# A first stage in sixteen groups of one K tile, finer attention preparation and another load order in a one-core mixer block

## The chip, the cores and the metric

The kernel runs on one core of one Trainium2 chip. The metric is the device time of one execution in microseconds; the kernel before takes 1273.27 us (median of three runs, 1273.0 to 1273.49). All times and rows in this document come from such runs and from the profile of one execution.

## What is computed

One layer of a hybrid block over 512 latent tokens that also reads 256 context tokens, all in 32-bit floats, width 2048:

```python
mod = silu(c) @ w_ada + b_ada                        # shift, scale, gate: 3 x 2048
h  = rms_norm(x, norm_w) * (1 + scale) + shift      # 512 tokens
hc = rms_norm(ctx, norm_w) * (1 + scale_c) + shift_c # 256 tokens, modulated by c_ctx
p, pc = h @ w_in, hc @ w_in                        # 6688 columns
# group A: gated delta rule, 8 heads, forward and backward scans in chunks of 64, after a short conv
# group B: attention, 8 query heads on 2 key heads, RMS norm of q and k, 2-D rotary positions
y = concat(gdn * silu(z_g), attn * silu(z_a)) @ w_out
out = rms_norm(x + gate * y, final_norm_w)
```

The modulation needs `shift` and `scale` before anything can be projected, and each of the sixteen K tiles (128 of the 2048 features) of `h` needs only its own 128 columns of `shift` and `scale`, but those columns over all 2048 rows of `w_ada`.

## The kernel before

Large products are made in three passes of rounded parts (`hi*hi`, `hi*lo`, `lo*hi`), so each weight piece is split by ScalarE (`hi`) and by GpSimd or VectorE (`lo`), and `h` is held as `hh` (high) and `hl` (low), with features on the partitions.

**First stage** (lines 307 to 567). The six token blocks of `ctx` and `x` are loaded (1 MB each), squared on ScalarE, turned by TensorE (`turn`, L363) and copied to `xts`. `ada(g)` (L388) makes shift and scale for a pair of K tiles: four 1 MB tiles `wada`, each filled by two transfers of 512 KB whose rows are 1 KB (256 columns), sixteen products of 512 columns (L404) into four column groups of 32 of the array, a copy (`part`, L409), four transposes (L413) and small VectorE steps into `md`. `make_h(g)` (L437) makes `hf = x * scale * 1/rms` (L446, VectorE), `hh` (L448, ScalarE) and `hl` (L450, VectorE) for both K tiles. `project(k)` (L463) adds one K tile to five accumulators (k, q of heads 0 and 1, v of head 0) in fifteen 512-column and nine 256-column passes, and yields after each of its five outputs. `gate_sums` (L453) adds the gate columns. The loop at L543 goes over eight groups of two K tiles: while group g is projected, `ada(g + 1)` and `make_h(g + 1)` are put into chosen slots of the ten. TensorE runs in the order in which this is written (`manual_schedule`); the other engines are ordered by the framework, SyncE issues all transfers in one queue. Six tiles of 1 MB (`big`) hold first the token blocks and then the `wada` pieces.

**Middle.** From the end of the first stage on, `pull(n)` puts about n columns of later projections on TensorE, between the links of other chains (L1228 to L1262). Then eight scans run, each with 35 slots; `prep_at` says at which slot the preparation of the next head goes on by one part. In the last scan `attn_prep` (L1044) is run in this way, at the slots of `LATE_AT`: fifteen parts that load, turn, normalise and rotate the keys, the values and the first query head. One part of it normalises and rotates a whole block on VectorE, and two scale a whole rotary table.

**Attention and output.** Thirteen `M` tiles are loaded, eight of the scans' outputs and then five z projections. In seventeen turns `u` the attention runs beside the z projection's fillers (`fill`) and the gate rows. `merged(i)` splits `M[i]` for the output product; all sixteen calls stand in the first output block.

```python
steps = ((3, 5, 6), (2, 5, 6), (2, 4, 5), (3, 5))[min(g, 3)]
sums = 0 if g + 1 == NG else steps[-1] if g < 2 else steps[0]
LATE_AT = dict.fromkeys((*range(1, 28, 2), 33), 1.5)
```

Of the kernel before, what the change touches and what calls it, by code (L numbers as in the profile page):

```python
# [17 lines left out]
D = 2048  # L18
# [4 lines left out]
NZA = 5  # L23
# [46 lines left out]
def build(tc, a):  # L70
# [23 lines left out]
    xts, hls = {}, {}  # L94
# [5 lines left out]

    def hl(m, k):
        return hls[m, k // 2][:, k % 2]
# [285 lines left out]
    def ada(g, halves=False):  # L388

        n, k0, rows = 2, 2 * g, 4  # L390
        md = mds[g] = p0.tile([128, 2, 2, 2], F32, tag="md", bufs=4, name=f"md{g}")

        def vec(v):
            return v[:, k0:k0 + n].unsqueeze(2).to_broadcast([128, n, 2])

        ada_ps = gtile([128, 512], f"ada{g}")
        for j in range(KT // rows):
            wt = big([128, rows, 2, 256], f"wada{g}_{j}")
            for s in range(2):
                src = w_ada[j * rows * 128:(j + 1) * rows * 128, s * D + k0 * 128:s * D + k0 * 128 + 256]  # L400
                SY.dma_start(wt[:, :, s], src.rearrange("(k p) c -> p k c", p=128))
            for r in range(rows):
                kk = j * rows + r
                T.matmul(ada_ps[32 * r:32 * r + 32], lhsT=cs[:, kk], rhs=wt[:, r].rearrange("p s c -> p (s c)"),  # L404
                         start=kk < 4, stop=kk >= KT - 4, skip_group_check=True)
            if j == 1 and halves:
                yield
        part = p0.tile([128, 512], F32, tag="part", bufs=2, name=f"part{g}")
        V.tensor_copy(part, ada_ps)  # L409
        yield  # L410
        tp = gtile([128, 4, 128], f"adat{g}")
        for i in range(4):
            T.transpose(out=tp[:, i], in_=part[:, i * 128:(i + 1) * 128], identity=ident)  # L413
        V.tensor_reduce(out=md.rearrange("p s i m -> p (s i) m"),
                        in_=tp.rearrange("p a (g m) -> p a m g", g=4)[:, :, 0:2], axis=AX.X, op=ALU.add)
        V.tensor_tensor(out=md[:, 0], in0=md[:, 0], in1=vec(vT), op=ALU.add)
        V.tensor_tensor(out=md[:, 1], in0=md[:, 1], in1=vec(b1), op=ALU.add)
        mul(V, md[:, 1], md[:, 1], vec(vT[:, 48:64]))

    wg = p0.tile([128, KT, 32], F32, name="wg")  # L420
# [14 lines left out]
    hfs = {}  # L435

    def make_h(p_):  # L437

        md = mds[p_]
        for m_ in range(2):  # L440
            hls[m_, p_] = low_tile(m_, p_, F32R, "h")
        for i in range(2):
            k = 2 * p_ + i
            hf = hfs[k] = p0.tile([128, NTOK], F32, tag="hf", bufs=3, name=f"hf{k}")
            for m_, t0, t1 in ((0, 0, SEQ), (1, SEQ, NTOK)):
                V.scalar_tensor_tensor(out=hf[:, t0:t1], in0=xts[m_, p_][:, i], scalar=md[:, 1, i, m_:m_ + 1],  # L446
                                       in1=rb[:, t0:t1], op0=ALU.mult, op1=ALU.mult)
                S.activation(hh[m_][:, k], hf[:, t0:t1], AF.Identity, bias=md[:, 0, i, m_:m_ + 1])  # L448
            for m_, t0, t1 in ((0, 0, SEQ), (1, SEQ, NTOK)):
                V.scalar_tensor_tensor(out=hl(m_, k), in0=hfs[k][:, t0:t1], scalar=md[:, 0, i, m_:m_ + 1],  # L450
                                       in1=hh[m_][:, k], op0=ALU.add, op1=ALU.subtract)

    def gate_sums(p_):  # L453

        for i in range(2):
            k = 2 * p_ + i
            for j in range(3):
                T.matmul(gps[32 * j:32 * j + 32], lhsT=wg[:, k], rhs=hfs[k][:, 256 * j:256 * j + 256],
                         start=False, stop=k == KT - 1, skip_group_check=True)
            T.matmul(gps[96:128, 0:2], lhsT=wg[:, k], rhs=mds[p_][:, 0, i], start=False, stop=k == KT - 1,  # L460
                     skip_group_check=True)
# [57 lines left out]
    for t in range(6):  # L519
        rds.append(turn(t))  # L520
        if t == 1:
            vec_columns()
        if t:
            spread(t - 1, rds[t - 1])
        if t == 4:
            first = ada(0, True)
            next(first)
    spread(5, rds[5])
    next(first)
    next(first, None)  # L530
    for k in range(2):
        first_weights(k)
    SY.dma_start(wg, w_in[:, COL_G:COL_G + 32].rearrange("(k p) c -> p k c", p=128))
    make_h(0)
# [8 lines left out]
    for g in range(NG):  # L543
        slot = 0
        ahead = ada(g + 1, g < 3) if g + 1 < NG else gates_in()
        steps = ((3, 5, 6), (2, 5, 6), (2, 4, 5), (3, 5))[min(g, 3)]
        sums = 0 if g + 1 == NG else steps[-1] if g < 2 else steps[0]
        for k in (2 * g, 2 * g + 1):
            if k + 2 < KT:
                first_weights(k + 2)  # L550
# [4 lines left out]
            for _ in project(k):  # L555
                if g + 1 < NG:
                    if slot in steps:
                        next(ahead, None)
                        if slot == steps[-1]:
                            make_h(g + 1)  # L560
# [1162 lines left out]
```

## Time and profile before

| | us |
|---|---|
| median of three runs | 1273.27 |
| the profiled execution | 1274.02 |
| its span, first to last instruction | 1271.9 |
| TensorE busy | 1235.5 (97%) |
| VectorE busy | 853.9 |
| ScalarE busy | 570.1 |
| first stage, to its last projection pass | about 158 |

The profile names an instruction by its line, its engine and the tiles that it writes and reads. PE is TensorE's matmul, PEld its weight load, DVE is VectorE, ACT ScalarE, POOL GpSimd, SP SyncE. A timeline row is: start in us, duration in us, engine, line, operation, output and inputs, shapes, count, and in brackets the idle time before it and what ended it. A busy PE isn't PE at its peak, since matmuls overlap: the distance between the starts of two passes is what a pass costs.

### The profile page before, as it was taken

Reading aid. Unit: us, or ns where it says so; the run is one execution under the profiler, and the core shown is the slowest. Engines: PE = TensorE matmul, PEld = TensorE weight load, DVE = VectorE, ACT = ScalarE, POOL = GpSimd, SP = SyncE. Lnnn points to the kernel's source line nnn. Section 1 sums busy time; section 2 is a strip of 40 time slices with the busy share of each in tenths; the row PEclk is TensorE's granted clock in tenths of the full one; section 3 lists DMA queues with packets and bytes.
Section 4 is the critical chain, followed back from the end, with each engine's and each line's share of the span. In section 5 each row is a group of like instructions: output and inputs, shape, how many; then the busy total and the mean of one; then the engine's idle time right before and its main releaser. Section 6 shows DMA issues by size and latency. Waiting matters only on the chain.

```text
span 1271.9 us, 24265 instructions
## 1 busy us (share of the span) xinstructions
PE 1235.5 (97%) x9242; PEld 1016.2 (80%) x9242; DVE 853.9 (67%) x1905; ACT 570.1 (45%) x1452; POOL 156.8 (12%) x206
## 2 busy tenths in 40 slices
PE   6899999999999999999999999999999999999997
PEld 4566788888888888888888887877888888787886
DVE  5444597596876778677786655547998997555433
ACT  5222373445545454454545444545555443434211
POOL 1222100111111111121211112200000000000000
PEclk9899999999999999999999999999999999999999
DMA  9999524132332223322233444357454443565202
GB/s 354 318 332 346 155 75 109 48 72 61 76 72 78 60 64 67 78 65 64 68 64 78 101 112 146 101 161 240 137 153 125 136 130 100 183 225 193 96 33 99
DMA packets 227287, 164.52 MB, mean 129 GB/s; under 512 B 62243, under 2 KB 198524, under 8 KB 226148
## 3 DMA queue, kind: packets, MB, share of 16 engines
q1 hardware_dynamic: 226874, 162.87, 44.1%
q8 instruction: 73, 1.20, 0.4%
q14 instruction: 43, 0.34, 0.1%
q10 hardware_dynamic: 297, 0.11, 0.0%
HBM read 148.85 MB, written 14.08 MB: 128 GB/s over the span
## 4 chain that ended last, share of the span: by engine, by line
PE 79%; DVE 10%; DMA 4%; ACT 3%; issue 3%; SPq 0%; POOL 0%; ACTq 0%; POOLq 0%; DVEq 0%
PE zl L1462 9%; PE kl L185 5%; PE ql L185 4%; PE vl L185 4%; PE po L148 3%; PE po L147 3%; PE po L149 3%; PE kvl L185 3%; PE tsh L972 3%; PE kx L185 2%; PE ada L404 2%; PE vx L185 2%; PE tsh L956 2%; PE klat L471 2%; PE pt L1391 2%
## 5 line engine op out<-in xcount | busy, mean ns | idle before, releaser
L960 ACT ACTIVATE vsh<-tsh,cch 128x128 f32<-128x128 f32 x88 | 32.4, 368 | 226.7 <-PE tsh L956 226.7
L289 POOL TENSOR_TENSOR sdh<-sth,egl 128x256 f32<-128x256 f32 x80 | 70.7, 884 | 445.2 <-DVE sth L978 364.3
L951 DVE SCALAR_TENSOR_TENSOR rh<-ksh,negeg,vtokh 64x128 f32<-64x128 f32 x176 | 61.2, 347 | 24.1 <-PE ksh L939 18.0
L148 PE MATMUL po<-wlo_wo,mh 128*128 128x512 f32 x192 | 76.1, 396 | 0.2 <-DVE wlo_wo L131 0.2
L147 PE MATMUL po<-whi_wo,mh 128*128 128x512 f32 x192 | 76.1, 397 | 0.0
L149 PE MATMUL po<-whi_wo,ml 128*128 128x512 f32 x192 | 76.0, 396 | 0.0
L1462 PE MATMUL zl<-hhL,whi_z 128*128 128x512 f32 x176 | 71.4, 405 | 0.0
L1462 PE MATMUL zl<-hL,whi_z 128*128 128x512 f32 x176 | 69.7, 396 | 0.0
L1462 PE MATMUL zl<-hhL,wlo_z 128*128 128x512 f32 x176 | 69.4, 395 | 0.0
L131 DVE TENSOR_TENSOR wlo_wo<-wraw_wo,whi_wo 128x512 fp32r<-128x512 f32 x48 | 33.0, 689 | 51.2 <-ACT whi_wo L130 51.1
L978 DVE TENSOR_TENSOR sth<-sdh,tsh 128x256 f32<-128x256 f32 x80 | 33.7, 421 | 44.0 <-PE tsh L972 35.7
L130 ACT CAST whi_wo<-wraw_wo 128x512 fp32r<-128x512 f32 x48 | 29.7, 618 | 57.8 <-PE po L149 47.5
L972 PE MATMUL tsh<-vsh,ktok 128*128 128x128 f32 x352 | 54.3, 277 | 0.4 <-ACT vsh L960 0.4
L972 PEld LDWEIGHTS tsh<-vsh,ktok 128*128 128x128 f32 x352 | 48.0, 191 | 3.5 <-ACT vsh L960 0.6
L1036 ACT CAST pth<-pt 128x512 fp32r<-128x512 f32 x48 | 26.5, 586 | 44.3 <-PE pt L1391 44.3
L185 PE MATMUL vl<-hhL,whi_v 128*128 128x512 f32 x112 | 46.3, 413 | 0.0
L967 ACT ACTIVATE oqh<-ksh,egsw 64x128 f32<-64x128 f32 x128 | 45.9, 358 | 0.8
L185 PE MATMUL vl<-hhL,wlo_v 128*128 128x512 f32 x112 | 46.2, 413 | 0.0
L185 PE MATMUL vl<-hL,whi_v 128*128 128x512 f32 x112 | 45.6, 408 | 0.0
L1510 DVE SCALAR_TENSOR_TENSOR gacc<-graw,scol,gacc 128x512 f32<-128x512 f32 x60 | 44.9, 748 | 1.1
L147 PEld LDWEIGHTS po<-whi_wo,mh 128*128 128x128 f32 x192 | 36.1, 188 | 9.6 <-ACT ze L1416 0.8
L148 PEld LDWEIGHTS po<-wlo_wo,mh 128*128 128x128 f32 x192 | 36.1, 188 | 9.2 <-DVE wlo_wo L131 0.6
(545 smaller groups left out, 3901.0 us busy)
## 6 DMA issues: line engine op xcount, KB each, us to landing
wada<-in_w_ada SPq DMA_DIRECT2D x64, 512.0 KB, 8.6
graw<-in_w_ada SPq DMA_DIRECT2D x64, 256.0 KB, 3.0
wraw_wo<-in_w_out SPq DMA_DIRECT2D x48, 256.0 KB, 3.0
wraw_z<-in_w_in SPq DMA_DIRECT2D x44, 256.0 KB, 3.0
wraw_v<-in_w_in SPq DMA_DIRECT2D x28, 256.0 KB, 3.1
wraw_k<-in_w_in SPq DMA_DIRECT2D x24, 256.0 KB, 2.9
wraw_q<-in_w_in SPq DMA_DIRECT2D x24, 256.0 KB, 2.8
xs<-in_x SPq DMA_DIRECT2D x4, 1024.0 KB, 8.4
```

What stands on the lines that cost most here:

```text
L131: (lo_eng or G).tensor_tensor(out=lo, in0=raw, in1=hi, op=ALU.subtract)
L147: T.matmul(out, lhsT=lh, rhs=rh, start=start, stop=False, skip_group_check=True)
L148: T.matmul(out, lhsT=lh, rhs=rl, start=False, stop=False, skip_group_check=True)
L149: T.matmul(out, lhsT=ll, rhs=rh, start=False, stop=stop, skip_group_check=True)
L185: T.matmul(out, lhsT=lw, rhs=rt[m], start=k == 0 and n == 0, stop=k == KT - 1 and n == 2, skip_group_check=True)
L289: eng.tensor_tensor(out=out, in0=x, in1=y, op=ALU.mult)
L951: behind["DVE"] = V.scalar_tensor_tensor(out=r[rows], in0=ks[rows, d], scalar=gsc["negeg"][rows, gcol:gcol + 1], in1=vtok[rows, p], op0=AL ...
L967: S.activation(oq[rows, v, p - 2], ks[rows, d], AF.Copy, scale=gsc["egsw"][rows, gcol:gcol + 1])
L972: T.matmul(ts[:, d], lhsT=ktok[:, p, half], rhs=vs, start=True, stop=True, skip_group_check=True)
L978: behind["DVE"] = V.tensor_tensor(out=sn, in0=sd, in1=ts[:, 0:2], op=ALU.add)
L1462: T.matmul(pl, lhsT=lw, rhs=rt, start=k == 0 and m == 0, stop=k == KT - 1 and m == 2, skip_group_check=True)
L1510: V.scalar_tensor_tensor(out=acc, in0=raw, scalar=scol[:, k:k + 1], in1=acc, op0=ALU.mult, op1=ALU.add)
```

## The change

The first stage goes over sixteen groups of one K tile. For each, two transfers of 1 MB bring the 128 columns of scale and then the 128 columns of shift, in rows of 512 bytes. `ada(k)` makes the scale first, and `hf` with it, and then the shift, `hh` and `hl`: two times sixteen products of 128 columns, two copies, two single transposes. The steps are taken one per slot of `project`, and `gate_sums` is called for each K tile. `hl` of K tile 0 gets tiles of its own (`spare`), the others move up by one half tile, and the squares' unused output goes to a part of `hhL`. The attention's preparation is cut into more parts at other slots, the rotary tables are scaled in parts of their own, and the loads stand further ahead of their use. The z tiles of `M` are loaded alternately with the others, `merged(0)` is called in turn 12, and three fillers are put ahead of the last turn's third transposition. Two `pull` amounts change.

```diff
+    spare = [pool_.tile([128, n], F32R, name=f"h{s}spare") for pool_, n, s in lows]
     def hl(m, k):
-        return hls[m, k // 2][:, k % 2]
+        if k == 0:
+            return spare[m]
+        g = (k - 1) // 2
...
-        junk = p0.tile([128, D], mybir.dt.bfloat16, tag="junk", bufs=1, name=f"junk{t}")
+        junk = hhL[:, 12:16].rearrange("p k t -> p (k t)")
...
+    def load_ada(k, s):
+        wt = big([128, KT, 128], f"wada{k}_{s}")
+        c0 = s * D + k * 128
+        SY.dma_start(wt, w_ada[:, c0:c0 + 128].rearrange("(k p) c -> p k c", p=128))
+        pieces[k, s] = wt
+    def ada(k):
+        md = mds[k] = p0.tile([128, 2, 2], F32, tag="md", bufs=4, name=f"md{k}")
+        bank = gtile([128, 4, 128], f"ada{k}")
+        for s in (1, 0):
+            wt = pieces.pop((k, s))
+            for kk in range(KT):
+                r = kk % 4
+                T.matmul(bank[32 * r:32 * r + 32, s], lhsT=cs[:, kk], rhs=wt[:, kk], start=kk < 4, stop=kk >= KT - 4,
+                         skip_group_check=True)
+            part = p0.tile([128, 128], F32, tag="part", bufs=2, name=f"part{k}_{s}")
+            V.tensor_copy(part, bank[:, s])
+            yield
+            tp = bank[:, 2 + s]
+            T.transpose(out=tp, in_=part, identity=ident)
+            V.tensor_reduce(out=md[:, s], in_=tp.rearrange("p (g m) -> p m g", g=4)[:, 0:2], axis=AX.X, op=ALU.add)
+            if s:
+                V.tensor_scalar(out=md[:, 1], in0=md[:, 1], scalar1=b1[:, k:k + 1], scalar2=vT[:, 48 + k:49 + k],
+                                op0=ALU.add, op1=ALU.mult)
+                hf = hfs[k] = p0.tile([128, NTOK], F32, tag="hf", bufs=3, name=f"hf{k}")
+                for m_, t0, t1 in SPANS:
+                    V.scalar_tensor_tensor(out=hf[:, t0:t1], in0=xts[m_, k // 2][:, k % 2], scalar=md[:, 1, m_:m_ + 1],
+                                           in1=rb[:, t0:t1], op0=ALU.mult, op1=ALU.mult)
+            else:
+                V.tensor_scalar(out=md[:, 0], in0=md[:, 0], scalar1=vT[:, k:k + 1], scalar2=None, op0=ALU.add)
+                for m_, t0, t1 in SPANS:
+                    S.activation(hh[m_][:, k], hfs[k][:, t0:t1], AF.Identity, bias=md[:, 0, m_:m_ + 1])
+                for m_, t0, t1 in SPANS:
+                    V.scalar_tensor_tensor(out=hl(m_, k), in0=hfs[k][:, t0:t1], scalar=md[:, 0, m_:m_ + 1],
+                                           in1=hh[m_][:, k], op0=ALU.add, op1=ALU.subtract)
+            yield
...
+    load_ada(0, 1)
+    first_weights(0)
+    load_ada(0, 0)
+    first = ada(0)
+    next(first)
     spread(5, rds[5])
+    load_ada(1, 1)
+    load_ada(1, 0)
+    first_weights(1)
     SY.dma_start(wg, w_in[:, COL_G:COL_G + 32].rearrange("(k p) c -> p k c", p=128))
+    load_ada(2, 1)
+    load_ada(2, 0)
+    for _ in first:
+        pass
+    load_ada(3, 1)
+    load_ada(3, 0)
...
+    events = (e for k in range(1, KT) for e in ada(k))
+    for k in range(KT):
+        if k + 2 < KT:
+            first_weights(k + 2)
...
+        if k and k + 3 < KT:
+            load_ada(k + 3, 1)
+            load_ada(k + 3, 0)
+        for slot, _ in enumerate(project(k)):
+            if k == KT - 1:
+                if slot == 0:
+                    gate_sums(k)
+                if slot in (1, 4):
+                    with tc.high_priority(offset=2500):
+                        next(last, None)
+                continue
+            if slot or k == 0:
+                next(events, None)
+            if k == 0 and slot == 4:
+                next(events, None)
+            if slot == 0 and k:
+                gate_sums(k - 1)
+            if k == KT - 2 and slot == 3:
+                gate_sums(k)
...
-    LATE_AT = dict.fromkeys((*range(1, 28, 2), 33), 1.5)
+    LATE_AT = dict.fromkeys((0, *range(4, 15), *range(16, 30), 31), 1.5)
...
-    pull(22000)
+    pull(25500)
...
-    for n in (5000, 5500, 0, 0, 5500, 0, 4000, 0, 0, 14000, 0, 0, 0, 0, 0):
+    for n in (2500, 5500, 0, 0, 5500, 0, 4000, 0, 0, 14000, 0, 0, 0, 0, 0):
...
     for i in range(8):
+        if i < NZA:
+            SY.dma_start(M[8 + i], zad[i])
         SY.dma_start(M[i], o_d[i])
-    for i in range(NZA):
-        SY.dma_start(M[8 + i], zad[i])
...
+        if h >= NH:
+            fill(3)
         if before is not None:
             pts.append(attn_pt(before[0], before[1], before[2], 2))
...
+        if u == 2 * NH - 4:
+            merged(0)
...
-            if first:
+            if first and k:
                 merged(k)
```

In `attn_prep` the parts of one key block are now, in this order: turn and square two blocks; turn and square four blocks and load the values; scale the cosine table (first block only); scale the sine table (first block only); normalise the context keys; normalise the latent keys and make the swapped product; turn the context values; finish the rotation; turn the latent values and load the next block; turn back the keys in two parts. The first query head follows in five parts and a last one for its transposition.

More of the change, by code (lines that the diff above doesn't have):

```diff
@@ L386, in build @@
     mds = {}
[L388 to L418, printed above, removed]
@@ new lines, in build @@
+    pieces = {}
+    def load_ada(k, s):
[33 more added lines that the diff above has]
+            yield
@@ L433, in first_weights, with gate_sums @@
         w0[k] = (hi[:, 0], vhi, hi[:, 1]), (lo[:, 0], vlo, lo[:, 1])
[L435 to L461, printed above, removed]
+    def gate_sums(k):
+        for j in range(3):
+            T.matmul(gps[32 * j:32 * j + 32], lhsT=wg[:, k], rhs=hfs[k][:, 256 * j:256 * j + 256],
+                     start=False, stop=k == KT - 1, skip_group_check=True)
+        T.matmul(gps[96:128, 0:2], lhsT=wg[:, k], rhs=mds[k][:, 0], start=False, stop=k == KT - 1,
+                 skip_group_check=True)
     def project(k):
@@ L1080, in attn_prep, with scaled @@
-        parts = ((0, 2), (2, 4))
+            jk = NT[:, 0:2].rearrange("p a b -> p (a b)")
+            for t in range(n):
+                S.activation(jk, tp[:, t], AF.Square, accum_out=ss[:, t:t + 1])
+            V.tensor_scalar(out=ss[:, :n], in0=ss[:, :n], scalar1=1.0 / 128.0, scalar2=EPS, op0=ALU.mult, op1=ALU.add)
+            power(ss[:, :n], -0.5)
+            return ss[:, :n].unsqueeze(2).to_broadcast([128, n, 128])
+        def scaled(out, tp, r):
+            V.tensor_tensor(out=out, in0=tp, in1=r, op=ALU.mult)
@@ L1081, in attn_prep, with rope_one, rope_two @@
+        def rope_one(y, tb, nm):
+            t2 = gp.tile([128, 6, 128], F32, tag="vtok", bufs=2, name=f"rt2{nm}")[:, :4]
+            mul(V, t2.rearrange("p t (a s r) -> p (t a) s r", a=2, s=2), swapped(y),
+                tb[:, 1].rearrange("p t (a s r) -> p (t a) s r", a=2, s=2))
+            return t2
+        def rope_two(y, tb, t2):
+            mul(V, y, y, tb[:, 0])
+            V.tensor_tensor(out=y, in0=y, in1=t2, op=ALU.add)
         kn = ktoks[0].rearrange("p a s d -> p (a s) d")
+        rope_load(tabk)
@@ L1470, in fillers, with merged @@
         z_over(*over)
+    def merged(i):
+        if i >= 1:
+            mh.append(mp.tile([128, SEQ], F32R, name=f"mh{i}"))
+            ml.append(mp.tile([128, SEQ], F32R, name=f"ml{i}"))
+        S.copy(mh[i], M[i])
+        V.tensor_tensor(out=ml[i], in0=M[i], in1=mh[i], op=ALU.subtract)
     def gate_bias(acc, row):
```

140 lines of the change are left out of this document (62 added, 78 removed).

## The prediction

> **What bounds the kernel now.** I read the page first, then a table of stretches (columns: length, busy time of PE, PEld, DVE, ACT, POOL with counts, granted TensorE clock, share of the 16 DMA engines, GB/s), then timelines.
>
> ```profile
> PE 1235.5 (97%) x9242; PEld 1016.2 (80%) x9242; DVE 853.9 (67%) x1905; ACT 570.1 (45%) x1452; POOL 156.8 (12%) x206
> ```
> ```profile
> 18.00:28.00 10.00, 7.01 (x44) 3.41 (x42) 5.76 (x21) 4.46 (x8) 2.08 (x4) 0.88 1.08 350
> 38.00:92.00 54.00, 52.62 (x321) 33.87 (x321) 24.93 (x46) 14.14 (x30) 14.37 (x14) 0.94 1.10 347
> 97.00:137.00 40.00, 39.27 (x256) 27.33 (x258) 20.49 (x43) 11.12 (x24) 12.45 (x11) 1.00 1.09 348
> 140.00:158.00 18.00, 18.00 (x121) 14.07 (x114) 9.81 (x27) 4.89 (x9) 1.64 (x10) 1.00 0.18 45
> 171.00:172.00 1.00, 1.00 (x9) 0.91 (x9) 0.47 (x2) 0.41 (x3) 0.00 (x0) 1.00 1.13 337
> ```
>
> TensorE is the bound after the first stage, so a hole removed there is time gained, and a stage that ends later costs its delay in full. In the first stage two things run level: the transfers flow at 347 GB/s from 38 to 137 us, and TensorE is busy at the same time. When the transfers have ended, 18 us of projection still follow. The stage runs from the first to the last of these two passes, 38.61 to 158.04 us, 119.4 us:
>
> ```profile
> 38.61 0.50 PE L471 MATMUL klat<-hhL,whi_w 128*128 128x512 f32 x1 [3.51 <-ACT hhL L448]
> ...
> 158.04 0.40 PE L185 MATMUL kvl<-hhL,whi_kv 128*128 128x512 f32 x1
> ```
>
> What does TensorE need in it? The timeline gives the price of each part.
>
> ```profile
> 60.47 0.40 PE L471 MATMUL qlat<-hhL,wlo_w 128*128 128x512 f32 x1
> 60.80 1.92 PE L404 MATMUL ada<-wada,cs 128*32 128x512 f32 x16
> ...
> 62.99 0.28 PE L473 MATMUL cctx<-hhC,w0h 128*128 128x256 f32 x1
> ...
> 113.64 0.60 PE L413 MATMUL adat<-cmain,part 128*128 128x128 f32 x4
> 114.00 0.48 PE L471 MATMUL klat<-hhL,whi_w 128*128 128x512 f32 x1
> ...
> 148.20 0.42 PE L458 MATMUL cctx<-hf,wg 128*32 128x256 f32 x3
> ...
> 149.53 0.28 PE L473 MATMUL cctx<-hhC,whi_w 128*128 128x256 f32 x1
> ...
> 152.80 0.40 PE L471 MATMUL klat<-hhL,whi_w 128*128 128x512 f32 x1
> ...
> 156.54 0.28 PE L473 MATMUL cctx<-hhC,w0l 128*128 128x256 f32 x1
> ```
> ```profile
> 107.36 3.64 PE L404 MATMUL ada<-wada,cs 128*32 128x512 f32 x32
> ```
>
> A projection: four of its five outputs take 152.80 to 156.66, 3.86 us, the fifth 0.70 (three passes 0.235 apart), so 4.56 us per K tile. A run of ada passes: 32 in 3.64 us on four column groups is 0.43 us for each 512-column pass of a group, 0.21 for 256, 0.107 for 128 if it scales. From the end of the qlat pass (60.47 + 0.235) to the moment the next cctx pass could have followed at the usual distance (62.99 - 0.235) are 2.05 us, of which 4 x 0.43 stream: **0.34 us go on changing from whole-array passes to column groups and back, whatever the run's length.** The gate sums show the same: 1.2 us to 149.3, of which 0.85 stream. Four transposes cost 0.43 us, 0.107 each, with no such loss.
>
> Now: 16 x 4.56 = 73.0; seven pairs of ada streaming 3.41 = 23.9; ten runs' changes 3.4 (the first three pairs are in two runs); gate sums 8 x 0.85 + four changes = 8.2 (four others join an ada run); transposes 3.0; the gates' own transposes 0.57. Together 112.1 us. The clock takes 3.1 us more:
>
> ```profile
> 40.00:50.00 10.00, 10.00 (x43) 7.10 (x44) 2.39 (x3) 1.64 (x5) 2.81 (x4) 0.69 1.10 351
> ```
>
> (10 x 0.31). So 4.2 of the 119.4 us are waits, the level race with the transfers.
>
> **The start of the stage.** Scale and shift of one K tile need 2 MB instead of 4 MB, and the sixth token block's turn no longer stands behind a wait for them.
>
> ```profile
> 21.66 2.07 DVE L372 COPY xL<-xt 128x256 f32<-128x256 f32 x6
> ...
> 27.56 2.66 PE L363 MATMUL xt<-cmain,xs 128*128 128x128 f32 x16
> ...
> 28.72 2.42 DVE L372 COPY xL<-xt 128x256 f32<-128x256 f32 x7 [2.96 <-PE xt L363]
> ```
> ```profile
> L446 DVE SCALAR_TENSOR_TENSOR hf<-xL,md,rb 128x512 f32<-128x512 f32 x16 | 12.1, 754 | 0.4
> L448 ACT ACTIVATE hhL<-hf,md 128x512 fp32r<-128x512 f32 x16 | 11.6, 723 | 29.7 <-DVE hf L446 29.7
> ```
>
> The turn that now starts at 27.56 can start when VectorE's copies let it, about 22.5; VectorE, free at 23.7, needs 2.4 for its copies and is done at 26.2. At 350 GB/s from 18 us on, the scale piece is there at 21.0 and, behind the first weights (0.33 MB), the shift piece at 24.9, about a microsecond more to land: neither is late. Then: copy of the scale sums (a quarter of a copy that now takes 0.69, I take 0.25), transpose, reduction and factor to about 27.2; hf 0.75 and about 0.5 to 28.5; copy, transpose, reduction and addition of the shift 0.9; hh 0.72: **the first projection at about 30.3 instead of 38.61, 8.3 us earlier** (29 to 32).
>
> **What TensorE does after it.** Projections 73.0. Ada: 30 runs (15 K tiles, scale and shift) of 8 passes per column group, 0.853 + 0.34 = 1.19 each, 35.7. Single transposes 30 x 0.107 = 3.2. Gate sums sixteen times alone, 0.43 + 0.34 = 0.77 each, 12.3. Gates 0.57. Together 124.8, 12.7 more than now: the streaming is the same, but 46 changes of the array's form are paid where 14 were. The slow clock lies between 0 and 3.1 (TensorE idles less ahead of the start, but not none): I take 2. Waits: between 1 and 6, I take 3. Of them about 1.5 because the third K tile's weights now stand behind two pieces of 1 MB (K tiles 2 and 3) in SyncE's queue, and ScalarE's and GpSimd's split follows; 0.5 for the gates' transposes, whose VectorE copies now have three slots instead of six; the rest for the copies behind hl on VectorE, whose steps per K tile sum to under 4 of some 8 us. Each step has one output, 0.70 to 1.05 us, between a run and its transpose.
>
> **End of the stage: 30.3 + 124.8 + 2 + 3 = 160.1 instead of 158.0, 2.1 us later.** The transfers don't set this. The row at 171 us, two loads of the attention's weights with rows of 512 bytes like the new pieces, ran at 337 GB/s where 1 KB rows give 347, so the 33.6 MB cost 99.6 instead of 96.7 us, 2.9 more, and end near 141; behind the last piece stand one run, three outputs, two gate sums, a projection and the gates, some 10.5 us: 151.5. The other bound for them is the last rival. The 1 MB size by itself I cost at nothing: several transfers are under way at any time, which keeps 347 GB/s up already. The squares' output in hhL costs nothing: that part is first written by K tile 12.
>
> **The later parts.** These are TensorE's holes, by the timeline:
>
> ```profile
> 170.15 1.03 PE L596 MATMUL gcp<-gg__116,ctri 128*128 128x6 f32 x8 [1.06 <-DVE gg__116 L589]
> ...
> 769.11 0.46 PE L956 MATMUL tsh<-rh,UU 128*128 128x128 f32 x2 [1.02 <-DVE rh L951]
> 779.82 0.44 PE L1041 MATMUL vtp<-cmain,kvch 128*128 128x128 f32 x2 [0.62 <-DMA kvch<-kvd]
> ...
> 805.91 0.44 PE L1041 MATMUL vtp<-cmain,kvch 128*128 128x128 f32 x2 [0.48 <-DMA kvch<-kvd]
> 828.40 0.46 PE L956 MATMUL tsh<-rh,UU 128*128 128x128 f32 x2 [0.89 <-DVE rh L951]
> ...
> 870.59 0.66 PE L1391 MATMUL pt<-cmain,pr 128*128 128x128 f32 x4 [0.83 <-ACT qn L1334]
> 873.73 0.66 PE L1391 MATMUL pt<-cmain,pr 128*128 128x128 f32 x4 [0.38 <-DVE ptl L1037]
> 884.92 1.31 PE L1391 MATMUL pt<-cmain,pr 128*128 128x128 f32 x8 [0.94 <-DVE pr L1383]
> ...
> 1070.38 0.65 PE L1391 MATMUL pt<-cmain,pr 128*128 128x128 f32 x4 [1.02 <-DVE ptl L1037]
> ```
> ```profile
> 869.43 0.63 ACT L1567 ACTIVATE zae<-M 128x512 f32<-128x512 f32 x1 [2.88 <-DMA M<-zad]
> ...
> 882.91 0.61 ACT L1599 CAST mh<-M 128x512 fp32r<-128x512 f32 x1
> ```
>
> *The pulls.* 3500 more columns (about 1.6 us) stand before the gates' product; the gates' last copies begin about a slot later against the stage's end. Of 1.06 us I take 0.5 (0 to 1.06).
> *The last scan.* Four holes, 3.0 us. Two end with the scan's step rh, late behind a rotary table's scaling or a whole normalisation on VectorE; with one such product or pair per part, nothing over some 1.4 us stands before rh. Two end with the load of the values; it is now issued three to five slots ahead of its use. I take 2.6 (1 to 3.0).
> *The attention.* The hole at 870.59 is ScalarE's: its tanh (869.43) waits 2.9 us for the z tile that is ninth in the queue, and the copy qn behind it holds a PSUM tile. Loaded first, the tile is there eight issues earlier; the next hole follows from the same. At 884.92 the split of M[0] (882.91, and its VectorE half behind it) had gone ahead of the softmax's product; it goes to turn 12, where it may cost a little. At 1070.38 three fillers cover the wait. Of 3.2 I take 2.7 (1.5 to 3.2). M[0] to M[4] move back by up to five issues in SyncE's queue; the first is split only at 882.91, 13 us behind the z tile's wait.
>
> **The sum,** against the profiled execution (1274.02: its span 1271.9 and 2.1 around it): 2.1 - 0.5 - 2.6 - 2.7 = -3.7, so 1270.3; that execution stands 0.75 above the median of the runs, so in their terms **1269.6**. Bounds of the terms: start 1.3 either way, clock -2 to +1, waits -2 to +3, the rest -1.5 to +3.3. Taken together, 1266.6 to 1272.6 is the forecast's own range. About 0.2% (2.5 us) is what a measurement can tell from no change.
>
> **The rivals.**
>
> *Weight loads show (slower).* Each short pass needs its own weight load:
>
> ```profile
> L404 PEld LDWEIGHTS ada<-wada,cs x256: 106/110/151, 22.8 to 139.2; 128*32 128x32 f32 x128
> ```
> ```profile
> 222.93 0.22 PE L854 MATMUL pxah<-DTh,grh 32*32 32x32 f32 x2 [0.22 <-DVE DTh L846]
> ...
> 223.74 0.21 PE L854 MATMUL pxah<-DTh,grh 32*32 32x32 f32 x2
> ```
>
> The load lasts 110 ns; under a 427 ns pass it vanishes, under 107 ns it may not. If loads and passes alternated, a run would stream 1.74 instead of 0.85 us, 30 runs +26 us. It turns the sign once a pass and its load cost more than 107 + 6.2/(30 x 8) = 133 ns. Against it: 96 small passes at 223 us, on four parts of the array, follow at about 34 ns per pass and part, so loads there overlap; that row is the nearest in length, the 110 ns the nearest in shape. At half the price: 1283.
> The Trainium skill, TensorE: Matmul & The Clock Gate, Part 3 (What overlaps and what doesn't), says that a weight load overlaps a running matmul only where the row groups differ; here all passes use all 128 rows, so by the page the whole 26 us would come, 1296. The trace disagrees at 512 columns: 32 passes in 3.64 us leave 0.2 us for all loads.
>
> *The transfers have the say (faster).* If the changes between forms are cheaper in short runs and the waits small, the stage ends where the transfers let it, 151.5, and the gain is 6.5 + 5.8: 1261. For it: stretches at 347 GB/s all along. Against it: the 0.34 shows in runs of 8, 16 and 32 passes.
>
> *The later parts don't do it (same).* The stage as forecast, but the smaller parts only move the waits for VectorE: 1274.9. For it: VectorE is busiest there; against it: each hole has one named cause that is moved.
>
> *Holes in the transfer queue (slower).* A transfer of 2048 packets (wg, the gate columns) is in the trace once, and what follows it is poor:
>
> ```profile
> 28.68 5.44 SPq L139 DMA_DIRECT2D wraw_w<-in_w_in  x1
> ```
> ```profile
> 34.00:35.00 1.00, 0.56 (x4) 0.42 (x4) 0.39 (x1) 0.85 (x3) 1.00 (x1) 1.00 0.36 49
> ```
>
> SyncE stood 5.4 us and a microsecond ran at 49 GB/s, 0.86 us of transfer lost. All 32 new pieces have 2048 packets. Such a hole after each would add 27.5 us to the transfers and end the stage near 179: 1288.5. Against it: these packets were of 128 bytes; of 512 bytes, two loads in a row kept 337.
>
> **How the numbers follow.** Forecast 0.44, weight loads 0.17, transfers 0.17, later parts 0.14, queue 0.08. Faster: 0.29 of the forecast and 0.16 of the transfers, 0.45. Same: 0.14, 0.01, 0.03 of the weight loads, 0.07 of the later parts, 0.25. Slower: 0.01 + 0.14 + 0.07 + 0.08 = 0.30. The range goes from just under the transfers' case to the half price of the weight loads, 1260 to 1284; the queue and the upper part of the weight loads stay out.
>
> **What would show it.** First klat pass near 30; ada runs of 32 passes with the next projection pass 1.1 to 1.2 us behind their start; the first kvl pass near 160; transfers thinning out before the end, since TensorE now paces them; no holes at the values' turns and at the first and last turns of the attention. Wrong if the ada runs last over 1.4 us, if the rate falls under 330 GB/s while pieces are wanted, or if rh is late again in the last scan.

## The result, and the profile after

The changed kernel takes **1281.31 us** (median of six runs, 1280.11 to 1283.08) beside 1273.38 us for the kernel before: ratio 1.0062, 95% interval 1.0049 to 1.0075. It is slower by 8 us where 3.7 us less had been forecast; the time lies inside the range, on the side of the rivals that lose. Its profiled execution has a span of 1278.9 us, 7.0 more than before.

Where the 7.0 us lie is read from three passes that stand at the borders of the stages: the first kvl pass (end of the first stage), the first zl pass (start of the attention) and the first po pass (start of the output product). The groups of the tiles zl and po, before and then after (duration shortest/median/longest in ns, first and last start in us):

```profile
L1462 PE MATMUL zl<-hhL,whi_z x176: 392/394/484, 860.3 to 1082.2; 128*128 128x512 f32 x176
...
L147 PE MATMUL po<-whi_wo,mh x192: 387/397/498, 1083.9 to 1218.5; 128*128 128x512 f32 x192
```
```profile
L1499 PE MATMUL zl<-hhL,whi_z x176: 392/394/484, 870.2 to 1088.5; 128*128 128x512 f32 x176
...
L154 PE MATMUL po<-whi_wo,mh x192: 389/397/500, 1090.3 to 1225.6; 128*128 128x512 f32 x192
```

With the first kvl pass at 158.04 before and 168.23 after (row below), the stretches are:

| stretch | before | after | difference | forecast |
|---|---|---|---|---|
| to the first kvl pass | 158.0 | 168.2 | +10.2 | +2.1 |
| from there to the first zl pass | 702.3 | 701.9 | -0.3 | -3.1 (pulls -0.5, last scan -2.6) |
| from there to the first po pass | 223.6 | 220.1 | -3.5 | -2.7 |
| from there to the end | 188.0 | 188.6 | +0.6 | 0 |

Two steps failed: the first stage, by 8 us, and the middle, by 3. The table of stretches of the first stage after the change, in the same stretches as shown of before (length, busy time of PE, PEld, DVE, ACT, POOL with counts, granted clock, share of the DMA engines, GB/s):

```profile
18.00:28.00 10.00, 6.74 (x70) 5.07 (x70) 8.67 (x28) 5.03 (x12) 2.91 (x5) 1.00 1.14 304
28.00:38.00 10.00, 7.57 (x79) 5.45 (x80) 3.89 (x12) 2.21 (x5) 1.29 (x2) 0.66 1.04 244
38.00:92.00 54.00, 50.62 (x588) 35.95 (x588) 24.52 (x63) 11.42 (x24) 11.11 (x14) 0.94 1.10 291
97.00:137.00 40.00, 38.75 (x462) 27.82 (x464) 21.51 (x55) 9.93 (x21) 9.64 (x10) 1.00 1.08 286
140.00:158.00 18.00, 17.89 (x215) 12.72 (x218) 7.96 (x22) 4.70 (x10) 3.54 (x5) 1.00 1.13 301
```

The last two columns matter most. The share of the DMA engines is as full as before (1.10), but they move 291 and 286 GB/s where they moved 347, and they are still at it from 140 to 158 us (301 GB/s), when before they had all but stopped (45 GB/s). The timeline of TensorE shows what follows from it:

```profile
28.20 0.46 PE L389 MATMUL rp<-rd,cmain 128*128 128x128 f32 x2 [2.52 <-DVE rd L383]
...
32.56 0.79 PE L469 MATMUL klat<-hhL,whi_w 128*128 128x512 f32 x1 [1.27 <-ACT hhL L430]
...
47.30 1.08 PE L412 MATMUL ada<-wada,cs 128*32 128x128 f32 x32
48.30 0.51 PE L469 MATMUL qlat<-hhL,whi_w 128*128 128x512 f32 x1
...
54.95 0.79 PE L469 MATMUL klat<-hhL,whi_w 128*128 128x512 f32 x1 [2.50 <-ACT whi_w L137]
...
128.39 1.08 PE L412 MATMUL ada<-wada,cs 128*32 128x128 f32 x32 [0.77 <-DMA wada<-in_w_ada]
...
136.90 1.08 PE L412 MATMUL ada<-wada,cs 128*32 128x128 f32 x32 [0.48 <-DMA wada<-in_w_ada]
...
157.92 1.08 PE L412 MATMUL ada<-wada,cs 128*32 128x128 f32 x32
...
168.23 0.50 PE L192 MATMUL kvl<-hhL,whi_kv 128*128 128x512 f32 x1
```

The runs at 128.39 and 136.90 wait for their piece, by under a microsecond each time; 8.5 us lie between them, in which one K tile's 2.43 MB come (two pieces of 1.05 MB and 0.33 MB of weights): 285 GB/s. From about 121 us on, then, the transfers set the pace, though PE is over 96% busy. Before that they don't: from 65.70 to 121.44 the K tiles start 7.96 us apart, as in the run rows_1k below, in which no piece is late, so this is TensorE's own pace. What it had lost by then it had lost around the third K tile, to the wait of 2.50 us at 54.95 and to a granted clock of 0.66 in the stretch around it:

```profile
52.00:62.00 10.00, 7.50 (x56) 4.77 (x55) 1.65 (x5) 1.63 (x4) 3.35 (x4) 0.66 1.02 279
```

From the start of the last run to the first kvl pass it is 10.3 us, as the prediction had it (10.5).

### The profile page after: what moved, and what is told of

Read it like the earlier page. It is cut to its first block, busy times and chain, and to the rows that moved or that the text cites. A ratio compares the mean times of both kernels' runs of the same rounds, so it can differ in the third digit from the quotient of the medians.

```text
span 1278.9 us, 25818 instructions
## 1 busy us (share of the span) xinstructions
PE 1244.0 (97%) x10010; PEld 1031.2 (81%) x10010; DVE 862.3 (67%) x1961; ACT 570.5 (45%) x1452; POOL 153.0 (12%) x206
## 4 chain that ended last, share of the span: by engine, by line
PE 70%; DVE 6%; issue 2%; ACT 2%; DMA 2%; SPq 0%; POOL 0%; ACTq 0%; POOLq 0%; DVEq 0%
PE zl L1499 8%; PE kl L192 5%; PE ql L192 4%; PE po L154 4%; PE po L155 4%; PE po L156 4%; PE vl L192 4%; PE tsh L980 3%; PE kx L192 3%; PE tsh L964 2%; PE vx L192 2%; PE pt L1428 2%; PE kvl L192 1%; PE ksh L945 1%; DVE cacc_q L255 1%
## 5 line engine op out<-in xcount | busy, mean ns | idle before, releaser
L986 DVE TENSOR_TENSOR sth<-sdh,tsh 128x256 f32<-128x256 f32 x80 | 33.6, 420 | 51.0 <-PE tsh L980 35.8
L1499 PE MATMUL zl<-hL,whi_z 128*128 128x512 f32 x165 | 65.4, 396 | 0.0
```

The costliest lines, as they stand in the source:

```text
L986: behind["DVE"] = V.tensor_tensor(out=sn, in0=sd, in1=ts[:, 0:2], op=ALU.add)
L1499: T.matmul(pl, lhsT=lw, rhs=rt, start=k == 0 and m == 0, stop=k == KT - 1 and m == 2, skip_group_check=True)
```

## Experiments

Theory 1, formed from these rows: the transfers' rate fell because of the rows of 512 bytes, the first stage ends 10 us late for that and nothing gives it back, while the later parts gain by themselves. The rivals are told with each run. All are compared with the kernel before on the same chip.

**The two halves of the change apart.** stage_only is the kernel before with the new first stage (everything of the diff up to the loop over K tiles); later_only is the kernel before with the new preparation, its slots, the load order, merged(0) and the fillers. Both keep the old pulls. The first and last lines of the two edits:

```diff
+    spare = [pool_.tile([128, n], F32R, name=f"h{s}spare") for pool_, n, s in lows]
...
+            if k == KT - 2 and slot == 3:
+                gate_sums(k)
```
```diff
+    LATE_AT = dict.fromkeys((0, *range(4, 15), *range(16, 30), 31), 1.5)
...
+        if i < NZA:
+            SY.dma_start(M[8 + i], zad[i])
...
+            if first and k:
                 merged(k)
```

> The change's first stage alone; preparation, load order and pulls as before. Theory 1: the stage ends 10 us later than before and nothing gives it back: about 1283.5 us; the hole of 2.8 us behind the first convolutions (a transpose waiting for VectorE's kq) comes from the smaller first number in the list of pulls and isn't there. Rival: the hole comes from the stage's late end, and the time is 1286 us or more.

> The kernel before with the later parts alone: 28 preparation parts for the attention, the z tiles ahead in the load order, the split of M[0] moved, three fillers in the last turns; first stage and pulls as before. Theory 1 (the later parts gain, the first stage loses): in the changed kernel the first zl pass stood 9.9 us later where the last kvl pass had stood 14.0 us later, and the first po pass 6.4 us later; so the later parts are worth about 4.1 + 3.4 - 0.7 = 6.8 us, and this kernel takes about 1266.6 us. Rival (the later stages only gave back delay that the first stage had brought, and gain nothing by themselves): 1272 to 1274 us.

stage_only takes 1283.17 us (ratio 1.0083, 1.0066 to 1.0099), later_only 1267.08 us (0.9958, 0.9943 to 0.9972). So the first stage loses 10.6 us and the later parts gain 5.4 us; the gain is their own. The two add up to +5.2, but the change costs +7.9. The remaining 2.7 us could belong to what both leave out, the pulls, but each of the three figures is known to about 2 us only, so the sum alone doesn't show it; the pulls are tried by themselves below. The groups of the kvl pass in stage_only, and its longest waits of the middle (total us, times, longest):

```profile
L192 PE MATMUL kvl<-hhL,whi_kv x64: 388/394/500, 168.4 to 696.5; 128*128 128x512 f32 x64
```
```profile
PE t1h L716 <- DVE kq L293: 1.0, 1, 1.0
PE gcp L604 <- DVE s_g L296: 0.9, 1, 0.9
```

The stage ends at 168.4, as in the changed kernel, and the hole ahead of t1h is 1.0 us.

**The length of the rows.** rows_1k is the changed kernel with each 1 MB piece read in rows of 1 KB; what the pieces hold is then the scale and shift of other features, so this kernel doesn't compute the reference's modulation.

```diff
-        c0 = s * D + k * 128
-        SY.dma_start(wt, w_ada[:, c0:c0 + 128].rearrange("(k p) c -> p k c", p=128))
+        c0, r0 = s * D + k // 2 * 256, k % 2 * 1024
+        SY.dma_start(wt.rearrange("p (k h) c -> p k (h c)", h=2),
+                     w_ada[r0:r0 + 1024, c0:c0 + 256].rearrange("(k p) c -> p k c", p=128))
```

> The changed kernel, but each 1 MB piece is read as 8 x 128 rows of 1 KB (256 neighbouring columns of half the rows) instead of 16 x 128 rows of 512 bytes. Tiles, buffers, transfers' size and number, instructions and their order stay; the scale and shift that are computed are not the reference's. Theory 1 (the rows' length sets the rate): the rate in the stage rises from 290 to about 345 GB/s, the transfers end near 141 us, and the stage's end is TensorE's, near 158 to 161 us instead of 168.2; the time falls by 8 to 10 us, to about 1272. Rival A (transfers of 1 MB that wait for six buffers set the rate): rate and time stay, 290 GB/s and 1281 us. Rival B (TensorE's changes of form set the end anyway): the rate rises, the stage still ends at 166 to 168 us, 1280 us.

```profile
28.00:38.00 10.00, 7.67 (x75) 5.22 (x75) 3.87 (x11) 2.19 (x5) 2.26 (x4) 0.52 1.00 283
38.00:92.00 54.00, 53.05 (x660) 38.57 (x661) 26.36 (x69) 12.00 (x26) 11.14 (x12) 0.99 1.10 350
...
140.00:158.00 18.00, 18.00 (x205) 12.60 (x193) 9.53 (x24) 5.00 (x11) 3.94 (x13) 1.00 0.12 31
```
```profile
L192 PE MATMUL kvl<-hhL,whi_kv x64: 392/394/628, 162.5 to 694.7; 128*128 128x512 f32 x64
```

These are the table of stretches and the group of kvl. The rate is 350 GB/s again, with the same 1 MB transfers, the same six buffers and the same work on TensorE; the transfers have ended before 140 us, and the stage ends at 162.5 instead of 168.2. The kernel takes 1274.59 us (1.0011, 1.0002 to 1.0021): 6.5 us less than the change, expected were 8 to 10. Rival A (transfers' size and buffers) and rival B (TensorE sets 166 to 168) fall. But the stage still ends 4.5 us later than before: that part is TensorE's.

Does the stage of the change end late because of the transfers, or because of what TensorE lost around the third K tile? stage_only, which has the same first stage, tells them apart. The starts of some K tiles (the first klat pass) in the three profiles, in us:

| | 4th | 10th | 12th | 14th | 16th | first kvl pass |
|---|---|---|---|---|---|---|
| rows_1k | 61.48 | 109.25 | 125.20 | 141.12 | 156.58 | 162.5 |
| the change | 65.70 | 113.44 | 130.24 | 146.88 | 162.35 | 168.2 |
| stage_only | 64.13 | 111.89 | 129.59 | 146.46 | 162.47 | 168.4 |

In stage_only the clock is 1.00 from 52 to 62 us, and up to the tenth K tile it is 1.6 us ahead of the change. Then its ada runs wait 3.0 us in five places (1.9 us of it for pieces, by the profile, the rest put down to VectorE's hL), where those of the change wait 1.2 us in two, and it ends no earlier. So what TensorE lost early only took the place of later waits: the transfers, whose share stays at 0.94 or more in every 8 us from 38 to 158 us in both, set the end.

rows_512 is the other way round, the kernel before with its transfers cut in two, for the rows alone:

```diff
-                src = w_ada[j * rows * 128:(j + 1) * rows * 128, s * D + k0 * 128:s * D + k0 * 128 + 256]
-                SY.dma_start(wt[:, :, s], src.rearrange("(k p) c -> p k c", p=128))
+                for i in range(2):
+                    c0 = s * D + (k0 + i) * 128
+                    src = w_ada[j * rows * 128:(j + 1) * rows * 128, c0:c0 + 128]
+                    SY.dma_start(wt[:, :, s, i * 128:i * 128 + 128], src.rearrange("(k p) c -> p k c", p=128))
```

> The kernel before, with each 512 KB transfer of scale or shift cut into two of 256 KB with rows of 512 bytes; tiles, TensorE's work and order as before. Theory 1 (the rows' length): the rate falls from 347 to about 292 GB/s, the 33.6 MB take 115 instead of 97 us and end near 155 us; the stage ends near 172 us and the time is 1286 to 1288 us. Rival (512-byte rows cost 3 per cent, as the two loads at 171 us had it; the size of the transfers or TensorE is the cause): 1273 to 1276 us.

```profile
38.00:92.00 54.00, 46.26 (x285) 28.11 (x286) 21.53 (x40) 12.16 (x26) 14.07 (x15) 0.91 1.10 289
...
140.00:158.00 18.00, 15.65 (x96) 10.60 (x100) 6.84 (x13) 3.77 (x8) 4.29 (x4) 0.91 1.14 300
```
```profile
PE ada L406 <- DMA wada<-in_w_ada: 13.4, 8, 2.6
```

289 GB/s, and now TensorE waits 13.4 us openly for the pieces: 1291.36 us (1.0144, 1.0124 to 1.0164). That is some 4 us more than expected: the first stage ends at 177.5, not at 172, and the rows show two contributions: the first K tile starts at 42.3 instead of 38.6, and the granted clock is 0.91 where the kernel before has 0.94 and 1.00. So rows of 512 bytes cost the old form of the stage 19 us and the new one 6.5. In the new form a part of the price is hidden behind TensorE's own later end (4.5 us with rows of 1 KB); whether its finer steps help too was not tried.

**Is it the gap or the row?** Neighbouring rows of a piece lie 24 KB apart in w_ada. near_512 takes the gap away: each piece is one unbroken MB, cut in the same 2048 rows of 512 bytes (again other features' values). rows_2k goes on from rows_1k to rows of 2 KB.

```diff
-        c0 = s * D + k * 128
-        SY.dma_start(wt, w_ada[:, c0:c0 + 128].rearrange("(k p) c -> p k c", p=128))
+        q0 = (2 * k + 1 - s) * 262144
+        SY.dma_start(wt, w_ada.rearrange("r c -> (r c)")[q0:q0 + 262144].rearrange("(k p c) -> p k c", p=128, c=128))
```

> The changed kernel, but each 1 MB piece is one unbroken MB of w_ada, cut into the same 2048 rows of 512 bytes with no gap between neighbours (in the changed kernel two rows lie 24 KB apart); everything else stays, and the scale and shift that are computed are not the reference's. Theory 1 (the price is that of a packet of 512 bytes, wherever it lies): the rate stays at 285 to 300 GB/s, the stage ends at 167 to 169 us, 1280 to 1282 us. Rival (the gap of 24 KB between short rows is what is slow): the rate rises towards 345 GB/s, the stage ends near 162.5 us as with rows of 1 KB, about 1275 us.

> As rows_1k, with rows of 2 KB (512 neighbouring columns of a quarter of the rows): scale and shift are again not the reference's. Theory 1 with the cost of a packet as a constant and a part that goes with its bytes (1 KB at 347, 8 KB at 425 GB/s: 0.62 ns and 2.28 ns per KB... that gives 287 GB/s at 512 bytes, where 292 was seen): about 388 GB/s at 2 KB while pieces are wanted. TensorE then sets the stage's end alone: it ends at 161 to 162.5 us, as with 1 KB, and the time is 1273 to 1275 us. Rival (with 1 KB rows the transfers still set the end): the stage ends 4 us or more earlier, near 158 us, and the time is 1270 us.

Two stretches and the page's packet line of near_512, and then of rows_2k:

```profile
DMA packets 210398, 164.62 MB, mean 129 GB/s; under 512 B 61731, under 2 KB 165244, under 8 KB 209252
...
38.00:92.00 54.00, 50.16 (x587) 35.51 (x587) 24.13 (x63) 11.31 (x24) 11.20 (x14) 0.94 1.04 294
97.00:137.00 40.00, 40.00 (x493) 28.93 (x492) 22.53 (x56) 9.92 (x21) 8.95 (x10) 1.00 1.03 292
```
```profile
DMA packets 210397, 164.62 MB, mean 130 GB/s; under 512 B 61730, under 2 KB 165243, under 8 KB 209251
...
38.00:78.00 40.00, 39.06 (x489) 28.16 (x487) 20.88 (x54) 9.17 (x20) 9.34 (x10) 1.00 1.05 382
...
140.00:158.00 18.00, 18.00 (x192) 12.62 (x191) 8.65 (x21) 4.67 (x9) 3.45 (x13) 1.00 0.15 35
```

near_512 stays at 292 to 294 GB/s and takes 1279.73 us (1.0049, 1.0033 to 1.0065): the gap is not the price. The pair shows more. The profile counts the same packets in both kernels, to within one, so where rows adjoin, four of them seem to count as one packet of 2 KB. Yet the one moves 292 and the other 382 GB/s (from 78 us on rows_2k moves less, since pieces are no longer wanted at once). What is left as a difference is how a row lands: 512 bytes in each of four partitions, or 2 KB in one. **In these runs the price follows the unbroken piece that lands in one partition, not the gap and not the packets that the page counts.**

rows_2k takes 1274.41 us (1.0007, 0.9997 to 1.0017), the same as rows_1k, and its stage ends at 161.4 us. With more transfer rate than TensorE can use, the new stage ends 3.4 us later than the old: TensorE's side of the change is a loss by itself.

**The pulls.** The list of pulls ahead of head 0's preparation begins with 2500 instead of 5000 columns in the change. In its trace, two rows of TensorE and one of VectorE (the gates' product, the transposition t1h, and what that waits for):

```profile
180.98 0.95 PE L604 MATMUL gcp<-gg__118,ctri 128*128 128x6 f32 x8
...
187.88 1.12 PE L716 MATMUL t1h<-cmain,kq 128*128 128x128 f32 x4 [2.83 <-DVE kq L293]
```
```profile
187.40 0.76 DVE L293 SCALAR_TENSOR_TENSOR kq<-craw,cacc_q 128x256 f32<-128x256 f32 x2
```

The hole of 1.06 us ahead of gcp has gone, as forecast. A larger one stands 7 us behind it: with 2500 columns fewer in front, the transposition comes before VectorE has finished head 0's q. prep_5000 undoes this one number:

```diff
-    for n in (2500, 5500, 0, 0, 5500, 0, 4000, 0, 0, 14000, 0, 0, 0, 0, 0):
+    for n in (5000, 5500, 0, 0, 5500, 0, 4000, 0, 0, 14000, 0, 0, 0, 0, 0):
```

> The changed kernel with the first number in the list of pulls ahead of head 0's preparation put back from 2500 to 5000 (the 25500 stays). Theory (the hole of 2.8 us at 187.88 is that number's doing: the transposes come before VectorE has convolved q): the hole shrinks to about 1 us or goes, and the time falls by 2 to 2.8 us, to 1278.5 to 1279.5 us. Rival (the hole belongs to the late end of the stage and only moves): 1281 us.

later_pull puts the larger pull on later_only, with the 5000 as before:

```diff
-    pull(22000)
+    pull(25500)
```

> The kernel before with the later parts (as later_only) and the one pull of 25500 instead of 22000 columns ahead of the gates' product. Theory: the hole of 1.06 us ahead of the gates' product goes, as in the changed kernel; 1 us less than later_only, about 1266 us. Rival: the 3500 columns are missing as cover further on, and the hole of 1 us ahead of head 0's transposes grows by as much: 1267 us.

prep_5000 takes 1275.98 us (1.0019, 1.0009 to 1.0029), 5.5 us less than the change by the ratios (some 2 us either way), twice what was expected. Its profiled execution is among its slower ones (2.3 us above the median; the first stage ends at 172.3), so the whole profiles are not compared, but the stretch from the first kvl to the first zl pass: 695.8 us, where the change has 701.9. Three parts of these 6.1 us are seen. The hole ahead of t1h shrinks to 1.8 us. The granted clock around it is 1.00 instead of 0.94, which is worth 1.7 us (the stretch from 171 to 200 us, of after and then of prep_5000):

```profile
171.00:200.00 29.00, 26.17 (x153) 21.97 (x152) 25.14 (x80) 21.52 (x54) 1.33 (x1) 0.94 0.22 65
```
```profile
171.00:200.00 29.00, 27.22 (x156) 22.70 (x155) 25.97 (x83) 22.10 (x55) 0.00 (x0) 1.00 0.24 65
```

And the scans wait less. The waits of TensorE from 230 to 700 us, of after and then of prep_5000:

```profile
PE tsh L964 <- DVE rh L959: 3.4, 6, 0.7
PE pxah L862 <- DVE DTh L854: 0.4, 1, 0.4
PE pxbh L870 <- issue: 0.3, 1, 0.3
```
```profile
PE tsh L964 <- DVE rh L959: 1.0, 4, 0.4
```

That is 3.1 us. So the same number also sets how the later projections meet the scans' VectorE steps, and this is no chance of one execution. The wait of tsh for rh there is 3.4 us in all four kernels with 25500 and 2500 columns (after, near_512, rows_1k, rows_2k), 0.8 to 1.0 in all four with 25500 and 5000 (prep_5000, later_pull, later_pull_2, early_start) and 1.8 to 2.0 in the five with 22000 and 5000. The stretch between the two passes goes with it: 700.4 to 701.9 us in the first four, 694.3 to 695.8 in the second. (The slow clock is not in all of the first: rows_2k has 1.00 and 700.4.) Why the meeting is better is not settled.

later_pull takes **1263.38 us** (0.992, 0.9905 to 0.9935), 10 us less than before: a version better than both. It had been expected to gain 1 us over later_only and gains 4.8. The profiles show the same parts again: the hole of 1.06 us ahead of gcp, the waits from 230 to 700 us (3.5 us in later_only, 1.2 in later_pull) and the clock from 171 to 200 us (0.94 and 1.00).

**Can the early start be kept?** early_start is later_pull with K tiles 0 and 1 done one at a time as in the change, and pairs with rows of 1 KB from K tile 2 on. later_pull_2 is later_pull once more, beside it. `ada_pair` is the old `ada` and `make_h` for one pair.

```diff
+    def chain():
+        yield from ada(1)
+        yield from ada_pair(1, True, loaded)
+        for g in range(2, NG):
+            yield from ada_pair(g, g < 4)
```

> The later parts and pulls of later_pull, but K tiles 0 and 1 loaded and computed one at a time as in the change (scale ahead of shift, 1 MB pieces, rows of 512 bytes), K tiles 2 to 15 in pairs with rows of 1 KB as before. Theory (the transfers set the pace of the first K tiles, so an early start is used up at the second pair): the first klat pass stands near 33 us instead of 38.9, the third K tile starts at 55 to 57.6 us (57.83 in later_pull, where the second pair's data sets it), and the stage ends at 156 to 158 us: 1262 to 1264 us. Rival (the early start is kept through the stage): the stage ends near 153 us, 1258 us.

> later_pull a second time, on the chip of the two others of this call: 1262.5 to 1264.5 us if the gain of 10 us is the kernel's and not the chip's or the day's.

```profile
33.98 0.80 PE L517 MATMUL klat<-hhL,whi_w 128*128 128x512 f32 x1 [1.28 <-ACT hhL L430]
...
53.17 1.07 PE L456 MATMUL adap<-wadap,cs 128*32 128x512 f32 x8 [0.31 <-DMA wadap<-in_w_ada]
60.32 0.79 PE L517 MATMUL klat<-hhL,whi_w 128*128 128x512 f32 x1 [4.32 <-ACT hhL L478]
```

early_start takes 1264.39 us (0.9933, 0.9919 to 0.9948), later_pull_2 1263.16 us (0.9927, 0.991 to 0.9944). TensorE starts 5 us earlier, at 33.98, but the second pair's last half arrives at 53.17 (51.59 in later_pull), and TensorE, with nothing ahead of them in its order, then waits 4.3 us for its copies, transposes and hh: the third K tile starts at 60.32 where it stands at 57.83 in later_pull. The stage ends at 160.1 (forecast 156 to 158). The rival falls: in this arrangement the early start is given back by the third K tile.

**The attention alone.** attn_only has the load order, merged(0) and the fillers, on the kernel before:

```diff
+        if i < NZA:
+            SY.dma_start(M[8 + i], zad[i])
         SY.dma_start(M[i], o_d[i])
...
+        if h >= NH:
+            fill(3)
...
+        if u == 2 * NH - 4:
+            merged(0)
```

> The kernel before with the attention's edits alone (z tiles ahead in the load order, the split of M[0] at turn 12, three fillers in the last turns). Theory (the attention's edits gain what the traces show, 223.6 to 219.8 us from the first zl to the first po pass, and give 0.7 us back in the output projection): about 3 us less than before, 1269.5 to 1271 us. Rival (the finer preparation of later_only made that gain by leaving other work ready): 1272.5 us or more.

It takes 1271.37 us (0.9989, 0.9979 to 0.9998): 1.4 us less, not 2.3 to 3.8. In its trace the stretch from zl to po is 219.9 us, 3.7 less than before, as the theory said, and the output product 0.6 more; but the stretches ahead of zl are 2.6 us longer than in the profile of before, with the same code there. Some 1.4 us of that is the execution that was profiled, 2.1 us above the median of its ten where that of before stands 0.8 above; the rest isn't settled. The stretch itself is steady: 219.8 to 220.3 us in all ten kernels with the attention's edits, 223.1 to 223.6 in the three without. So the attention's gain is 1.4 us by the times and 3.1 by the stretches.

## Why the prediction was wrong, step by step

**The transfers' price: this step failed.** The prediction let TensorE alone set the stage's end: "The transfers don't set this." Its reason was the price: "The row at 171 us ... ran at 337 GB/s where 1 KB rows give 347, so the 33.6 MB cost 99.6 instead of 96.7 us." The row was one microsecond of a burst of 0.5 MB; over 54 us (38 to 92) the pieces in rows of that length, with the weights between them, move 289 to 294 GB/s in after, near_512 and rows_512. Why the burst stood higher isn't settled. At 290 GB/s the 33.6 MB cost 116 us, and the stage by the transfers, 151.5 in the prediction, becomes 168: that is where it ended. A better row was in the same trace, the stretch of the kernel before in which the x blocks come, 1 MB each with rows of 8 KB:

```profile
10.00:18.00 8.00, 7.56 (x54) 6.52 (x53) 7.31 (x29) 7.42 (x13) 0.68 (x2) 1.00 1.02 425
```

425 GB/s for 8 KB and 347 for 1 KB are 19.3 and 2.95 ns a row. A line through these two, so much for a row (0.62 ns) and so much for its bytes (2.28 ns for each 1000), gives 287 GB/s at 512 bytes and 388 at 2 KB; measured are 286 to 294 and 382. The line is a fit, which the two lengths bear out (388 stands in the expectation of rows_2k), not a mechanism that was shown. The sign that was named, a rate under 330 GB/s while pieces are wanted, is the one that came.

The Trainium skill, DMA: Bandwidth & Descriptors, Specifications, has 512 bytes as enough for the full line rate; the trace disagrees, 292 beside 350 GB/s. The same page, Why small descriptors are slow (HBM only), gives a fixed overhead of about 3 cycles for each packet beside one cycle for each 32 bytes; an estimate from it would be 347 x (16/19) / (32/35) = 320 at 512 bytes, in the right direction but too little by half.

**TensorE's sum was right.** Of the 124.8 us plus 5 for clock and waits, rows_1k shows 128.8 (33.7 to 162.5). The run at 47.30 stands between these two passes:

```profile
47.09 0.28 PE L471 MATMUL cctx<-hhC,wlo_w 128*128 128x256 f32 x1
...
48.65 0.40 PE L469 MATMUL qlat<-hL,whi_w 128*128 128x512 f32 x1
```

Measured as the prediction did, with the usual distances taken off at both ends (from 47.09 + 0.12 to 48.65 - 0.235), the run costs 1.21 us; 1.19 was forecast. From its start to the start of the next pass it is 1.0. The gate sums (0.75) and the tail (10.3) were as worked out too. Only "the streaming is the same" is not quite so: 1.7 of the 12.7 us are K tile 1's sums, which had run ahead of the start. So the rival of the weight loads falls: in four column groups, eight loads of 110 ns and eight passes of 107 each fit into the 1.21 us, where they would take 1.74 one after another. By the Trainium skill, TensorE: Matmul & The Clock Gate, Part 3 (What overlaps and what doesn't), these loads would not overlap the passes, all on the same 128 rows; the trace disagrees for these short passes too. That the extra changes of the array's form cost more than the early start brings is what rows_2k shows: 161.4 beside 158.0 with transfers out of the way.

**The start: mis-sized.** 30.3 was forecast, bounds 29 to 32; the first pass came at 32.56. VectorE's copies were done at 26.1, as worked out, but the next two rows had been left out of the sum:

```profile
26.78 1.27 DVE L383 TENSOR_SCALAR rd<-cmain,ssx 128x128 f32<-128x128 f32 x1 [0.66 <-POOL ssx L290]
27.97 0.28 DVE L415 COPY part<-ada 128x128 f32<-128x128 f32 x1
```

The last block's 1/rms goes through GpSimd (0.66) and takes VectorE 1.27 us, and only behind it comes the copy of the scale's sums.

**Clock and waits: mis-sized.** Behind the start the clock cost 2.4 us up to 38 us and 3.4 more from 52 to 62, 5.8 where 2 were taken:

```profile
32.56:38.00 5.44, 5.44 (x43) 4.09 (x44) 1.42 (x3) 1.17 (x3) 0.90 (x1) 0.56 0.95 204
```

TensorE's waits in the list are 4.6 us, where 3 were taken. With the late start these terms, 32.56 + 124.8 + 5.8 + 4.6, come to 167.8, close to the 168.2 that were measured, but they are not the reason for the late end: in stage_only the clock behind the start costs 3.0 us instead of 5.8, longer waits for pieces take its place, and the stage ends at 168.4.

**The third K tile's weights** behind two 1 MB pieces: 1.5 was forecast, 2.50 measured (54.95), by the mechanism named. With rows of 1 KB the wait is gone, so it too is a price of the rows.

**The pulls: this step failed as well.** The prediction priced the 3500 columns more ahead of gcp (0.5 of 1.06; all of it went, and with the 5000 kept it gains 4.8) and didn't price the 2500 fewer three lines further on. That number costs 5.5 us (prep_5000 against the change): the hole ahead of t1h, the slower clock behind it and the waits in the scans, none of which stands in the sum.

**The last scan** was right in its mechanism: the waits of 3.0 us that were listed there are gone from the list of waits, down to one row from 700 to 870 us:

```profile
PE tsh L964 <- DVE rh L959: 0.5, 2, 0.2
```

The gain of the whole stretch from kvl to zl (0.3) is smaller since the pulls' loss lies in it too; in later_only, with the old pulls, it is 1.7 (700.6 us), less than the 2.6 forecast, though kernels with the same code there differ by 2 us (701.5 to 703.7 with the old preparation and pulls). So the rival that the later parts only move the waits falls.

**The attention** was right, 3.5 beside 2.7, of which the output product gives 0.6 back; the rows of pt at 879.01 and 881.99 have no hole, and the one for the softmax's product is down from 0.94 to 0.38:

```profile
879.01 1.04 PE L1428 MATMUL pt<-cmain,pr 128*128 128x128 f32 x8
881.99 0.60 PE L1428 MATMUL pt<-cmain,pr 128*128 128x128 f32 x4
...
892.56 1.32 PE L1428 MATMUL pt<-cmain,pr 128*128 128x128 f32 x8 [0.38 <-DVE pr L1420]
```

The rival "transfers have the say" had the right resource and the wrong sign, since it went by 347 GB/s; the rival of holes in the queue was right that the short rows would make the transfers late, but no such hole follows each piece: in stretches of 8 us the rate lies between 260 and 301 GB/s from 38 to 158 us.

## What to carry to other kernels

When a change makes the rows of a transfer shorter, price them by a line through two sustained rates at other row lengths, not by a short burst; and when two resources run level, work out the stage by each of them with the pessimistic price. A gain at the front of a stage is worth only what its slowest supply leaves of it, and an engine that looks busy and has few waits can still be held by that supply at the end. Test each number of a hand-tuned schedule by itself: of two pull amounts one gained 4.8 us and the other lost 5.5.

## What was not expected of the hardware

Pieces that land as 512 bytes, 1 KB and 2 KB in one partition move at 286 to 294, 350 and 382 GB/s, with the DMA engines' share at 1.03 to 1.14 in all of them, and this doesn't change when the rows lie side by side in memory and the profile counts as many packets as with rows of 2 KB. The share of busy DMA engines therefore doesn't tell a good transfer from a bad one; the GB/s beside it do.
